# Side-by-side merges and one pass per head in a neighbourhood-attention and delta-rule layer

## The chip, the cores and the metric

The kernel runs on one core of a Trainium2 chip. The metric is device time in microseconds (us), the median of several runs. Inside the core PE is the matrix engine (TensorE), PEld its loading of the stationary operand, DVE the vector engine, ACT the scalar engine, POOL the GpSimd engine, and SP the queue that issues nearly all DMAs. PSUM is the accumulator memory that PE writes; it has eight banks of 512 floats in each of 128 partitions. L701 is line 701 of the kernel.

## What is computed

One layer over 1024 latent tokens (a grid of 16 rows by 64 columns) of width 1024, with 256 context tokens. The projection `w_in` is 1024 x 4112, the output projection `w_out` 1024 x 1024, all in float32. The reference, cut to what matters and with its einsums shortened (`hc` is projected in the same way and gives the context's keys, values and chunks):

```python
h  = rmsnorm(x, g_pre) * (1.0 + scale[:, None]) + shift[:, None]
hc = rmsnorm(xc, g_pre) * (1.0 + scale_c) + shift_c
na_q, na_k, na_v, na_z, g_qkv, g_z, g_b, g_a = jnp.split(h @ w_in, IN_SPLITS, axis=-1)
...

# neighbourhood attention, 8 heads of 64, for each row r of the grid:
s_loc = jnp.einsum('bchd,bicjhd->bhcij', q_r, k_win) + bias      # a window of 8 x 16 keys
s_ctx = jnp.einsum('bchd,bnhd->bhcn', q_r, k_ctx)                # all 256 context keys
p = jax.nn.softmax(jnp.concatenate([s_loc, s_ctx], axis=-1), axis=-1)
o_na = p_loc . v_win + p_ctx . v_ctx

# gated delta rule, 4 heads of 128, both directions, the context's chunks first:
t_inv = triangular_solve(eye + a, eye)                           # one inverse for each chunk
v_new = u_n - w_n @ state
o_n   = q_n @ state + qk_n @ v_new
state = state * gl_n + k_n^T @ v_new

y = jnp.concatenate([o_na * silu(na_z), rmsnorm(o_g, gdn_norm_w) * silu(g_z)], -1) @ w_out
return x + gate[:, None] * rmsnorm(y, g_post)
```

## The kernel before

The kernel is one program in four stages.

**Front.** Norm and modulation of `x`, the projections that the delta rule needs, its convolutions, and the first groups of small inverses. The change does not touch it.

**Projections and merges (`phase_a2`).** The rest of the `w_in` projections run on PE as products of two-part operands: each float32 matrix is held as a high part in the fast float32 format and a low part, and a product is three matmuls (high by high, low by high, high by low). The generator `fill` issues them, `pz` (the gates) last. Beside it two other generators are advanced by turns: `blocks` (the last group of 32 x 32 inverses) and `merges`. For each of the four heads `inv_merge` builds the inverse of 10 chunks of 128 in both directions `d` from four 32 x 32 inverses each. It loads the off-diagonal blocks `pm` and the small inverses `vd`, transposes `vd` into `ld`, copies the small inverses to the diagonal of the zeroed results `tm[0]` and `tm[1]` (and into `xo`), and then does two levels of "multiply, copy from PSUM, multiply, negate into place": `tz` (L1108), `zt`, `tu` (L1122) on blocks of 32, and `tz2` (L1136), `z2`, `tu2` (L1142, L1144) on blocks of 64. At the end both `tm` are stored to `tm_dram`. A head is done before the next begins. There are three `tm` buffers and each head takes two, so from head 1 on a `tm` has to wait for a store of the head before. Even heads put `pm` into the buffers `kk0`, `kk1` of the pool `pf`, in which the first pair of attention heads will be held; so `blocks` waits for all four merges (`len(ready) < 4`) before it issues the load of that pair.

**Attention and scan (`phase_b`).** Attention works on 4 pairs of heads x 2 row tiles `rt` x 4 column tiles `ct`, two heads `hh` each: 64 heads' tiles of 128 queries. `na_scores` adds bias and mask to `gm` on POOL (L729), puts the scores of the context into a PSUM tile `pc` (L736) and those of the neighbourhood's rows into another, `pl` (L739); each has its bank, with two buffers. DVE takes the maximum over `pc` (L744) and then, in one custom pass over `pl` and `gm` (L745), writes the biased scores and extends the maximum; ACT does the two exponentials with their sums (L746, L747). `na_turn` transposes the weights back into the same PSUM tiles (L754, L758), ACT copies `tcx` (L756), DVE copies `tl` (L760). `na_values` accumulates `po` (L769, L774). Between the steps of attention the delta rule's scan (`delta_step`, 4 heads x 10 chunks) is advanced by a fixed ratio. PE's order here is fixed: `self.pe` ties every matmul to the one before. The other engines' orders come from a scheduler that follows the order of the program.

**Output projection (`phase4`).** `w_out` is loaded in eight rows of 128 x 1024 in the order `W_ORDER`, in halves (`wor`), and each half is split into a high part on ACT and a low part on POOL (L701). That begins during attention: `w_out_early` takes over buffers that attention and the scan have finished with, four rows ahead. `m` is the gated result, in eight rows too. The products (L1337, L1338, L1339) go row by row over seven PSUM tiles. `last` holds the scan's end for head 3 (`delta_end`: normalisation at L1284, four transposes `ot` at L1287, twice).

The lines that set the orders and buffers that the prediction speaks of:

```python
W_ORDER = [3, 0, 1, 2, 4, 5, 6, 7]
...
tm = [g3.tile([P, 10, P], F32, name=f"tm{h}_{d}", tag="tm", bufs=3) for d in range(2)]
...
while done < min(118, (i + 1) * 118 // 130):
    next(sc)
...
banks = {"sc": 2, "sl": 2, "po": 1, "pa0": 1, "pa1": 1, "os": 1}
```

## Time and profile before

| | |
|---|---|
| median of 3 runs | 890.77 us |
| the three runs | 889.36, 890.77, 899.58 us |
| the profiled execution | 898.68 us, of which its span is 896.9 |
| mean granted PE clock | 0.962 |
| moved by DMA | 160.97 MB, mean 179 GB/s |

How to read the rows that follow. The page gives for each engine its busy time, its share of the span and the number of its instructions; then the span in 40 slices, with the busy tenths of each slice and under `PEclk` the tenths of full clock that PE was granted. A table of stretches has start and end in us, the length, then busy time and count of PE, PEld, DVE, ACT and POOL, then PE's busy share, its clock and what the DMAs moved in GB/s (the prediction names the last columns where it uses them). The chain of waits has start, length, engine and operation, in order of time, followed back from the last instruction. A group of instructions has line, engine, operation, output and inputs, shapes and count, then busy us, mean ns of one, and the idle time of the engine just ahead of them with what ended most of it. A wait has who waited, for whom, the us, the number of waits, and the longest.

The kernel's time by stages: the front to 460 us, projections and merges to 556, attention and scan to 797, output projection to the end at 897.

### The profile page before, as it was taken

Reading aid. Unit: us, or ns where it says so; the run is one execution under the profiler, and the core shown is the slowest. Engines: PE = TensorE matmul, PEld = TensorE weight load, DVE = VectorE, ACT = ScalarE, POOL = GpSimd, SP = SyncE. Lnnn points to the kernel's source line nnn. Section 1 sums busy time; section 2 is a strip of 40 time slices with the busy share of each in tenths; the row PEclk is TensorE's granted clock in tenths of the full one; section 3 lists DMA queues with packets and bytes.
Section 4 is the critical chain, followed back from the end, with each engine's and each line's share of the span. In section 5 each row is a group of like instructions: output and inputs, shape, how many; then the busy total and the mean of one; then the engine's idle time right before and its main releaser. Section 6 shows DMA issues by size and latency. Waiting matters only on the chain.

```text
span 896.9 us, 16578 instructions
## 1 busy us (share of the span) xinstructions
PE 837.1 (93%) x6082; PEld 704.4 (79%) x6082; DVE 542.1 (60%) x1179; ACT 416.9 (46%) x1165; POOL 352.8 (39%) x415
## 2 busy tenths in 40 slices
PE   6999999999999979898989997899899999989996
PEld 4678887888788858688877876788788888868885
DVE  3453454556536699779649433577677787781332
ACT  4253535745653554563143533556455555661210
POOL 1333221734453442345512112646546566643110
PEclk9899999999999999999998986799999999989999
DMA  9687442265365535743899857978829523251251
GB/s 339 248 284 253 131 127 85 83 217 169 106 200 174 151 100 176 196 107 93 299 259 253 214 189 288 347 169 217 301 77 294 160 80 133 71 193 66 96 183 51
DMA packets 95175, 160.97 MB, mean 179 GB/s; under 512 B 28581, under 2 KB 55542, under 8 KB 92918
## 3 DMA queue, kind: packets, MB, share of 16 engines
q1 hardware_dynamic: 87606, 146.25, 52.5%
q10 hardware_dynamic: 7488, 13.67, 4.9%
q8 instruction: 48, 0.79, 0.4%
q14 instruction: 33, 0.27, 0.1%
HBM read 110.82 MB, written 52.42 MB: 182 GB/s over the span
## 4 chain that ended last, share of the span: by engine, by line
PE 61%; DVE 19%; DMA 11%; ACT 3%; issue 3%; SPq 2%; POOL 1%; DVEq 0%; POOLq 0%; ACTq 0%
PE py L1337 3%; PE py L1339 3%; PE py L1338 3%; DVE tb L1063 3%; DVE vb L1066 3%; PE pz L461 2%; PE pz L465 2%; PE pz L466 2%; DMA pm_dram<-pm 2%; PE pl L739 2%; PE po L774 2%; PE po L769 2%; PE pa L1228 2%; PE pc L736 2%; DMA tm_dram<-tm 2%
## 5 line engine op out<-in xcount | busy, mean ns | idle before, releaser
L729 POOL TENSOR_TENSOR gm<-gt,mk 128x288 f32<-128x288 f32 (+1 forms) x48 | 46.3, 969 | 40.4 <-DVE nm L745 40.4
L1204 POOL TENSOR_SCALAR kd<-kt,kd 128x128 f32<-128x128 f32 x72 | 42.7, 604 | 28.0 <-PE pa L1239 27.9
L746 ACT ACTIVATE pt<-pt,nm 128x288 f32<-128x288 f32 (+1 forms) x64 | 36.7, 574 | 30.2 <-DVE nm L745 29.9
L760 DVE COPY tl<-pl 96x384 f32<-96x384 f32 (+1 forms) x64 | 35.3, 552 | 17.3 <-PE pl L758 16.4
L745 DVE CUSTOM_DVE_ANT_0 pt<-pl,gm,mi 128x288 f32<-128x288 f32 (+1 forms) x64 | 36.3, 567 | 11.0 <-POOL gm L729 4.7
L1005 ACT ACTIVATE em<-em,gc 128x128 f32<-128x128 f32 x80 | 25.6, 391 | 34.3 <-DMA em<-gc_dram 29.3
L465 PE MATMUL pz<-hl,wh_gz 128*128 128x512 f32 x96 | 39.9, 415 | 0.0
L466 PE MATMUL pz<-hh,wl_gz 128*128 128x512 f32 x96 | 39.5, 412 | 0.0
L461 PE MATMUL pz<-hh,wh_gz 128*128 128x512 f32 x96 | 39.4, 410 | 0.0
L474 PE MATMUL pv<-wh_nv,hh 128*128 128x264 f32 x128 | 35.7, 298 | 2.0 <-ACT hh L263 1.6
L1208 POOL TENSOR_SCALAR vb<-v,beta 128x128 f32<-128x128 f32 x40 | 24.2, 606 | 32.6 <-DVE y L1212 16.7
L475 PE MATMUL pv<-wh_nv,hl 128*128 128x264 f32 x128 | 36.9, 293 | 0.0
L476 PE MATMUL pv<-wl_nv,hh 128*128 128x264 f32 x128 | 35.9, 290 | 1.0 <-DVE wl_nv L447 1.0
L1391 ACT ACTIVATE finv<-py 128x512 f32<-128x512 f32 x16 | 9.6, 599 | 57.3 <-PE py L1339 39.1
L1063 DVE TENSOR_TENSOR tb<-ab,vb 120x31 f32<-120x31 f32 (+15 forms) x62 | 30.2, 487 | 9.9 <-DMA ab<-ab_dram 8.3
L872 DVE SCALAR_TENSOR_TENSOR acc_v<-xp_v,cols,acc_v 128x1282 f32<-128x1282 f32 x16 | 29.1, 1818 | 10.9 <-ACT acc_v L870 10.6
L1392 DVE TENSOR_TENSOR finv<-py,ggb 128x512 f32<-128x512 f32 x16 | 11.0, 690 | 40.6 <-ACT finv L1391 40.5
L744 DVE TENSOR_REDUCE mi<-pc 128x1 f32<-128x256 f32 x64 | 26.9, 420 | 12.4 <-PE pc L736 11.6
L1024 POOL TENSOR_SCALAR_AFFINE_SELECT qe<-qe 128x256 f32<-128x256 f32 x32 | 24.2, 759 | 24.7 <-DVE qe L1023 24.3
L758 PE MATMUL pl<-c,pt 128*96 128x128 f32 (+1 forms) x192 | 32.1, 277 | 0.0
L1020 DVE SCALAR_TENSOR_TENSOR pm<-pk,beta,em 128x128 f32<-128x128 f32 x80 | 23.6, 343 | 13.1 <-PE pk L1013 10.9
L872 DVE SCALAR_TENSOR_TENSOR acc_q<-xp_q,cols,acc_q 128x1024 f32<-128x1024 f32 x16 | 20.5, 1284 | 17.0 <-ACT acc_q L870 16.7
(433 smaller groups left out, 2907.5 us busy)
## 6 DMA issues: line engine op xcount, KB each, us to landing
wada<-in_w_ada SPq DMA_DIRECT2D x16, 512.0 KB, 6.9
em<-gc_dram SPq DMA_DIRECT2D x20, 256.0 KB, 4.1
pm_dram<-pm SPq DMA_DIRECT2D x20, 256.0 KB, 3.2
pmf<-pm_dram SPq DMA_DIRECT2D x8, 640.0 KB, 7.0
tm_dram<-tm SPq DMA_DIRECT2D x8, 640.0 KB, 7.5
kk<-qk_dram SPq DMA_DIRECT2D x16, 320.0 KB, 9.1
tm<-tm_dram SPq DMA_DIRECT2D x4, 1280.0 KB, 16.1
kq_dram<-kq SPq DMA_DIRECT2D x4, 1152.0 KB
```

The lines of the kernel that those rows point to most:

```text
L461: r = nc.tensor.matmul(ps, wh, xh, start=(k == 0), stop=False)
L465: nc.tensor.matmul(ps, wh, xl, start=False, stop=False)
L466: nc.tensor.matmul(ps, wl, xh, start=False, stop=(k == KC - 1))
L474: nc.tensor.matmul(ps, xh, wh, start=(k == 0), stop=False)
L475: nc.tensor.matmul(ps, xl, wh, start=False, stop=False)
L476: nc.tensor.matmul(ps, xh, wl, start=False, stop=(k == KC - 1))
L729: nc.gpsimd.tensor_tensor(self.gm[hh][:, :n].rearrange("p (n c r) -> p n c r", c=nco, r=4), gv, self.mk[:, mo:mo + n].rearrange("p (n c r) ...
L745: nc.vector.tensor_tensor_reduce(pt[:, :n], pl[:, :n], gm[:, :n], -1.0, mi, ALU.add, ALU.min, nm)
L746: nc.scalar.activation(pt[:, :n], pt[:, :n], AF.Exp, bias=nm, scale=-1.0, accum_out=sums[:, ct, hh, 0:1])
L872: nc.vector.scalar_tensor_tensor(av, xp[:, s0 + tap:s0 + tap + 1282 - s0], wc(tap), av, ALU.mult, ALU.add)
L1063: nc.vector.tensor_tensor(t3, bc(ab[:, 0:m, m:m + 1], [r, m, n]), bc(vb[:, m:m + 1, m:], [r, m, n]), ALU.mult)
L1204: nc.gpsimd.tensor_scalar(kd[d], kt_[:, t, :], self.kd[:, h, d, t:t + 1], None, ALU.mult)
```

## The change

Four things are changed together.

1. **Merges side by side.** `inv_merge` is cut into five stages, and the table `MERGES` interleaves the stages of neighbouring heads. `tm[1]` is allocated a stage later than `tm[0]`, its four diagonal copies go from ACT to POOL, and the order of the copies changes. For even heads `ld`, `xo`, `zt` are now also put into the first pair's buffers (`ql0`, `qh1`, `ql1`) beside `pm` in `kk0`, `kk1`. The first pair's load is issued when three merges are done. The ring of `tm` stays at three.
2. **One pass per head.** Scores of rows and context lie side by side in one PSUM tile of two banks, rows ending at column 512 and context behind it, two buffers. One custom DVE pass runs over both (288 + 256 or 384 + 256 columns); the separate maximum is gone. `gm` becomes three lasting tiles with zeros under the context's columns. One exponential with one sum replaces two. All five transposes are issued ahead of the copies. `tcx` and `tl` have three buffers instead of four.
3. **The start of the scan.** The first step's `kd` and `vb` on POOL are ordered behind the `gm` issued by then, and the scan is advanced by `1 + max(0, i - 2) * 117 // 127` steps instead of `(i + 1) * 118 // 130`.
4. **The output projection's start.** `W_ORDER` begins with row 0. Rows 0 and 3 of `w_out` and row 0 of `m` are split during attention into the first pair's buffers, row 1 of `w_out` into `o` and `tm`: three rows of `w_out` ahead instead of four. A piece is split at the earliest two steps after it was issued for loading (`clock`). The scan's end is issued at the third row of products instead of the fifth.

```diff
@@ -134,7 +134,9 @@
-W_ORDER = [3, 0, 1, 2, 4, 5, 6, 7]
+MERGES = [(0, 0), (0, 1), (1, 0), (0, 2), (1, 1), (0, 3), (0, 4), (2, 0), (1, 2), (2, 1), (1, 3), (1, 4), (3, 0), (2, 2), (3, 1),
+          (2, 3), (2, 4), (3, 2), (3, 3), (3, 4)]
+W_ORDER = [0, 3, 1, 2, 4, 5, 6, 7]
...
@@ -607,6 +609,9 @@
+        self.gms, self.gmi = [self.nw.tile([P, 640], F32, name=f"gm{i}") for i in range(3)], 0
+        for g in self.gms:
+            nc.gpsimd.memset(g[:, 384:], 0.0)
...
@@ -644,15 +647,21 @@
             if p == 2:
-                self.wait_w = 6
-                self.w_out_early(self.pf, [("qh0", 8), ("ql0", 8), ("qh1", 8), ("ql1", 8), ("kk0", 10), ("kk1", 10)])
+                self.clock += 4
+                w = [self.pf.tile([P, n], F32, name=f"early_{t}", tag=t)[:, :D]
+                     for t, n in (("qh0", S), ("ql0", S), ("qh1", S), ("ql1", S), ("kk0", S + CT), ("kk1", S + CT))]
+                self.split_w(W_ORDER[0], *w[:2])
+                self.split_w(W_ORDER[1], *w[2:4])
+                self.ms[0] = tuple(v.bitcast(F32R) for v in w[4:])
+                self.split_later(self.m_dram[0:P, :], *w[4:])
+                self.clock -= 4
...
@@ -665,38 +674,33 @@
-            self.split_piece()
+            self.split_piece(1, 2)
...
+    def split_piece(self, n=1, wait=0):
+        nc = self.nc
+        self.clock += 1
+        for _ in range(n):
+            if not self.staged or self.clock - self.staged[0][0] < wait:
+                return
+            _, raw, hi, lo = self.staged.pop(0)
             self.order(nc.scalar.copy(hi.bitcast(F32R), raw), self.last_exp)
             nc.gpsimd.tensor_tensor(lo.bitcast(F32R), raw, hi, ALU.subtract)
             self.load_pieces()
@@ -725,39 +729,39 @@
         if ct != 2:
-            self.gm[hh] = self.nw.tile([P, 384], F32, name=f"gm{p}_{u}_{hh}", tag="gm", bufs=3)
-            nc.gpsimd.tensor_tensor(self.gm[hh][:, :n].rearrange("p (n c r) -> p n c r", c=nco, r=4), gv,
+            self.gm[hh] = self.gms[self.gmi % 3]
+            self.gmi += 1
+            r = nc.gpsimd.tensor_tensor(self.gm[hh][:, 384 - n:384].rearrange("p (n c r) -> p n c r", c=nco, r=4), gv,
                                     self.mk[:, mo:mo + n].rearrange("p (n c r) -> p n c r", c=nco, r=4), ALU.add)
+            self.last_gm = r.ins.name
         gm = self.gm[hh]
-        pc = ps.tile([P, 512], F32, name=f"pc{p}_{u}_{hh}", tag="sc", bufs=2)[:, :256]
-        pl = ps.tile([P, 512], F32, name=f"pl{p}_{u}_{hh}", tag="sl", bufs=2)
+
+        sc = ps.tile([P, 1024], F32, name=f"sc{p}_{u}_{hh}", tag="sc", bufs=2)
+        pl, pc = sc[:, :512], sc[:, 512:768]
...
-            self.pe(nc.tensor.matmul(pl[:, :n].rearrange("p (n f) -> p n f", f=m), a[:, u * P:(u + 1) * P], kv,
+            self.pe(nc.tensor.matmul(pl[:, 512 - n:].rearrange("p (n f) -> p n f", f=m), a[:, u * P:(u + 1) * P], kv,
                                      start=(i == 0), stop=(i == 1)))
-        mi = self.nw.tile([P, 1], F32, name=f"mi{p}_{u}_{hh}", tag="mi", bufs=4)
...
-        nc.vector.tensor_reduce(mi, pc, AX.X, ALU.max, negate=True)
-        nc.vector.tensor_tensor_reduce(pt[:, :n], pl[:, :n], gm[:, :n], -1.0, mi, ALU.add, ALU.min, nm)
-        nc.scalar.activation(pt[:, :n], pt[:, :n], AF.Exp, bias=nm, scale=-1.0, accum_out=sums[:, ct, hh, 0:1])
-        self.last_exp = nc.scalar.activation(pt[:, 384:640], pc, AF.Exp, bias=nm,
-                                             accum_out=sums[:, ct, hh, 1:2]).ins.name
+        nc.vector.tensor_tensor_reduce(pt[:, 384 - n:], sc[:, 512 - n:768], gm[:, 384 - n:], -1.0, 3.0e38, ALU.add, ALU.min, nm)
+        self.last_exp = nc.scalar.activation(pt[:, 384 - n:], pt[:, 384 - n:], AF.Exp, bias=nm, scale=-1.0,
+                                             accum_out=sums[:, ct, hh:hh + 1]).ins.name
...
     def na_turn(self, nm, m, pc, pl, pt):
...
-        tcx = self.nw.tile([P, 2, P], F32, name=f"tcx{nm}", tag="tcx", bufs=4)
+        for rc in range(3):
+            self.pe(nc.tensor.transpose(pl[:m, (rc + 1) * P:(rc + 2) * P], pt[:, 384 + (rc - 3) * m:384 + (rc - 2) * m], self.ident))
+        tcx = self.nw.tile([P, 2, P], F32, name=f"tcx{nm}", tag="tcx", bufs=3)
...
@@ -1072,34 +1076,35 @@
     def inv_merge(self, g3, ps, h):
...
+        pm = [buf(f"pmf{d}_", f"pm{d}", [10, P], f"kk{d}") for d in range(2)]
...
-        tm = [g3.tile([P, 10, P], F32, name=f"tm{h}_{d}", tag="tm", bufs=3) for d in range(2)]
...
+        yield
+
+        ld, xo, zt = buf("ld", "ld", [2, 10, 32], "ql0"), buf("xo", "xo", [10, 64], "qh1"), buf("zt", "zt", [2, 10, 32], "ql1")
+        tm = [g3.tile([P, 10, P], F32, name=f"tm{h}_0", tag="tm", bufs=3)]
         nc.gpsimd.memset(xo, 0.0)
-        yield
+        nc.gpsimd.memset(tm[0], 0.0)
...
         yield
+        tm.append(g3.tile([P, 10, P], F32, name=f"tm{h}_1", tag="tm", bufs=3))
+        nc.gpsimd.memset(tm[1], 0.0)
+        for b in range(4):
+            sl = slice(32 * b, 32 * b + 32)
+            nc.gpsimd.tensor_copy(tm[1][sl, :, sl], ld[sl, 1])
...
-        yield
         for d in range(2):
             nc.sync.dma_start(self.tm_dram[h][:, d], tm[d])
+        yield
...
@@ -1183,7 +1200,10 @@
                 if (h, i) == (3, 1):
-                    self.w_out_early(g3, [("o", 8), ("tm", 20)])
+                    w = [g3.tile([P, n, P], F32, name=f"early_{t}", tag=t, bufs=2).rearrange("p t c -> p (t c)")
+                         for t, n in (("o", 8), ("tm", 20))]
+                    self.spare = w[1][:, D:2 * D]
+                    self.split_w(W_ORDER[2], w[0], w[1][:, :D])
...
+                if (h, i) == (0, 0):
+                    self.order(r, self.last_gm)
...
-        banks = {"sc": 2, "sl": 2, "po": 1, "pa0": 1, "pa1": 1, "os": 1}
-        tags = [tag for tag, n in banks.items() for _ in range(n)]
+        tags = ["sc", "sc", "sc", "sc", "po", "pa0", "pa1", "os"]
...
                     next(parts, None)
+                    self.split_piece(2)
+                    if i == 2:
+                        for _ in last:
+                            pass
...
-                    if i == 4:
-                        for _ in last:
-                            pass
-                        self.split_piece(6)
...
-                while len(ready) < 4:
+                while len(ready) < 3:
...
+                heads = [self.inv_merge(ap, ps, h) for h in range(4)]
+                for h, stage in MERGES:
+                    while stage == 0 and (8 * h + 7) // 12 not in self.yd:
                         yield
-                    yield from self.inv_merge(ap, ps, h)
-                    ready.append(h)
+                    next(heads[h])
+                    if stage == 4:
+                        ready.append(h)
...
-                    while done < min(118, (i + 1) * 118 // 130):
+                    while done < min(118, 1 + max(0, i - 2) * 117 // 127):
```

What that does to the order of instructions is shown at three places. The first is PE at the end of the projections. Before, the rows around the last projection matmul (`pz_1`, L466), and then, after head 3's `tu`, those up to the first scores (`pc`, L736); `pmf_0` and `pmf_1` are head 3's off-diagonal blocks, `z` its `z2`:

```order
L466 MATMUL pz_1_5673<-hh,wl_gz_4_5640 128x512
L1122 MATMUL tu_0_5369<-vd_5297,zt_5322 32x32
...
L1136 MATMUL tz_00_5469<-xo_5305,pmf_0_5293 64x64 x5
L1136 MATMUL tz_05_5476<-xo_5305,pmf_0_5293 64x64 x5
L1136 MATMUL tz_10_5483<-tm_1_5304,pmf_1_5295 64x64 x5
L1142 MATMUL tu_00_5497<-tm_0_5303,z_5468 64x64 x5
L1136 MATMUL tz_15_5490<-tm_1_5304,pmf_1_5295 64x64 x5
L1144 MATMUL tu_10_5498<-z_5468,xo_5305 64x64 x5
L1142 MATMUL tu_05_5511<-tm_0_5303,z_5468 64x64 x5
L1144 MATMUL tu_15_5512<-z_5468,xo_5305 64x64 x5
L736 MATMUL pc_0_0_5723<-kk_0_5266,qh_0_5269 128x256
```

After, the last projection is L468, and `pmf_2` are head 2's blocks:

```order
L468 MATMUL pz_1_5673<-hh,wl_gz_4_5640 128x512
L1153 MATMUL tz_00_5262<-xo_4897,pmf_2_4766 64x64 x5
L1159 MATMUL tu_00_5290<-tm_0_4899,z_5261 64x64 x5
...
L1161 MATMUL tu_15_5305<-z_5261,xo_4897 64x64 x5
L1139 MATMUL tu_0_5326<-vd_5092,zt_5173 32x32
L1139 MATMUL tu_0_5326<-zt_5173,vd_5092 32x32
...
L1153 MATMUL tz_00_5438<-xo_5172,pmf_3_5088 64x64 x5
...
L1161 MATMUL tu_15_5481<-z_5437,xo_5172 64x64 x5
L743 MATMUL sc_0_0_5728<-kk_0_5061,qh_0_5064 128x256
```

Before, only head 3's second half stands behind the last projection. Now the second half of head 2 stands there too, and behind it head 3's from `tu` (L1139) on; head 2 ends in the middle.

The second place is POOL at the start of attention. Before, with `vb` and `kd` the operands of the scan's first steps and `gm` the bias tiles of attention:

```order
L1091 MEMSET tm_1_5304 128x1280
L1208 TENSOR_SCALAR vb_1_1_5774<-v_5737,beta 128x128
L1208 TENSOR_SCALAR vb_1_0_5819<-v_5737,beta 128x128
L1208 TENSOR_SCALAR vb_1_9_5887<-v_5737,beta 128x128
L1204 TENSOR_SCALAR kd_0_0_5770<-kt_5738,kd 128x128
L1204 TENSOR_SCALAR kd_1_1_5772<-kt_5738,kd 128x128
L1204 TENSOR_SCALAR kd_0_1_5812<-kt_5738,kd 128x128
L729 TENSOR_TENSOR gm_0_0_5721<-gt_0_5284,mk 128x288
```

After, from the zeroing of head 3's second `tm` on:

```order
L1127 MEMSET tm_1_5320 128x1280
L1130 COPY tm_1_5320<-ld_5171 32x10x32 x4
L614 MEMSET gm_5718 128x256
L614 MEMSET gm_5719 128x256
L614 MEMSET gm_5720 128x256
L734 TENSOR_TENSOR gm_5718<-gt_0_5079,mk 128x288
L734 TENSOR_TENSOR gm_5719<-gt_1_5081,mk 128x288
L734 TENSOR_TENSOR gm_5720<-gt_0_5079,mk 128x384
L1224 TENSOR_SCALAR kd_0_0_5785<-kt_5739,kd 128x128
L1224 TENSOR_SCALAR kd_1_1_5787<-kt_5739,kd 128x128
L1230 TENSOR_SCALAR vb_1_1_5789<-v_5738,beta 128x128
```

The first three `gm` went ahead of the scan's operands, and the copies into head 3's `tm[1]` and three short memsets came in ahead of them.

The third place is PE at the start of the output projection. Before, from the last scan product (`pos`, L1250) to the first product of the projection (`py`, L1337):

```order
L1250 MATMUL pos_8485<-vn_0_9_9085,qe_7703 128x128
L1250 MATMUL pos_8485<-vn_1_2_9088,qe_7703 128x128
L754 MATMUL pc_7_1_9042<-c_60,pt_7_1_9050 128x128 x2
L758 MATMUL pl_7_1_9043<-c_60,pt_7_1_9050 96x128 x3
L769 MATMUL po_1_8844<-tcx_7_1_9104,vcx 64x128
...
L774 MATMUL po_1_8844<-tl_7_0_9080,vv_7632 64x128
L637 MATMUL prt_1_9139<-c_60,rb_1_9137 128x128 x4
L1287 MATMUL ot_0_9295<-c_60,o_8314 128x128 x4
L1337 MATMUL py_0_9167<-wo_o_8360,m_9145 128x512
```

After:

```order
L1274 MATMUL pos_8250<-vn_0_9_8780,qe_7534 128x128
L1361 MATMUL py_1_8866<-early_qh_8151,early_kk_8155 128x512
L1362 MATMUL py_1_8866<-early_qh_8151,early_kk_8156 128x512
L1363 MATMUL py_1_8866<-early_ql_8152,early_kk_8155 128x512
L1274 MATMUL pos_8250<-vn_1_2_8783,qe_7534 128x128
L758 MATMUL sc_7_1_8743<-c_60,pt_7_1_8749 128x128 x2
L760 MATMUL sc_7_1_8743<-c_60,pt_7_1_8749 96x128 x3
L1361 MATMUL py_0_8867<-early_qh_8151,early_kk_8155 128x512
...
L778 MATMUL po_1_8565<-tl_7_0_8777,vv_7440 64x128
...
L640 MATMUL prt_1_8833<-c_60,rb_1_8831 128x128 x4
L1311 MATMUL ot_0_8960<-c_60,o_8076 128x128 x4
```

The first products, of row 0 (`early_qh`, `early_ql`, with `early_kk` as `m`), now stand between the last scan products, the last transposes and the scan's end, and the two `ot` follow each other closely.

99 lines of the change are left out of this document (46 added, 53 removed).

## The prediction

> **What bounds the kernel now.** I read the page's totals and slices first, then a table of stretches, then the chain of waits in order of time, then the groups by form, and last the timeline at the seams.
>
> ```profile
> span 896.9 us, 16578 instructions
> PE 837.1 (93%) x6082; PEld 704.4 (79%) x6082; DVE 542.1 (60%) x1179; ACT 416.9 (46%) x1165; POOL 352.8 (39%) x415
> PEclk9899999999999999999998986799999999989999
> ```
>
> PE is busy nearly throughout, and the only dip of its clock lies in the slices between about 500 and 580 us. The table of stretches (length; busy time and count of each engine; clock; DMA) shows the seams:
>
> ```profile
> 460.00:542.00 82.00, 76.93 (x1114) 62.59 (x1113) 47.90 (x103) 38.47 (x84) 13.02 (x12) 0.90 0.81 228
> 542.00:556.00 14.00, 9.60 (x203) 8.93 (x202) 5.24 (x11) 4.10 (x9) 1.17 (x1) 0.64 0.65 233
> 556.00:571.00 15.00, 9.99 (x54) 9.38 (x55) 6.07 (x18) 4.99 (x18) 9.97 (x14) 0.54 1.01 400
> 571.00:797.00 226.00, 209.74 (x1927) 186.96 (x1923) 171.12 (x532) 133.65 (x490) 132.87 (x179) 0.99 0.60 175
> 797.00:885.00 88.00, 88.00 (x373) 71.15 (x374) 34.20 (x47) 19.84 (x43) 15.62 (x21) 0.97 0.35 121
> ```
>
> The last projections and the merges end at 542, a tail of merges runs to 556, attention starts at half clock, runs to 797, and the output projection follows without a gap. So what can be won is: the tail and the start (29 us at a clock of 0.64 and 0.54), the weight loader's idle time in attention (226 - 187 = 39 us), and the seam at 790 to 805. The work before 440 us is not touched.
>
> **The merges.** The chain in order of time (start, length, what), from the end of head 0 to the first scores:
>
> ```profile
> 489.69 0.79 PE tu L1142 x10
> ...
> 496.87 1.39 PE tu L1122 x100
> ...
> 500.07 0.23 PE pk L461
> ...
> 501.70 1.30 PE tz L1136 x20
> ...
> 514.00 9.28 DMA tm_dram<-tm
> ...
> 537.64 4.99 DMA tm_dram<-tm
> ...
> 542.74 1.18 POOL tm L1091
> 543.93 0.46 ACT tm L1099
> ...
> 545.83 0.61 ACT st_z L553
> ...
> 547.06 0.47 DVE tm L1127
> ...
> 548.19 3.11 PE tz L1136 x27
> ...
> 555.70 0.72 PE pc L736 x2
> ```
>
> Each head ends with the store of its `tm`, and a later head's `tm` waits for that store, since there are three buffers. Head 2's store at 537.64 is followed by the memset, four copies, the negations and two passes until 555.70: 18.1 us for one handover. Heads 0 and 1 end at about 491 and 513.
>
> The new order runs heads 0 and 1 together, then 2 and 3, but the ring still has three buffers in the same roles: head 2's second `tm` waits for head 1's store, head 3's for head 2's. In PE's order head 0 ends after 22 more projection matmuls (22 x 0.23 = 5.1 us) and beside head 1's first passes, where it had waited before; I put its end at 495. From there to head 1's end stand 75 projection matmuls (17.3 us) and passes of about 4 us; with 2 us of waits, 518. Then two handovers follow with only 15 projection matmuls between them. One costs: the store, 5.0 to 9.3 us by the two rows, taken as 7 because `kk` and `ql` loads are now issued just ahead of it; the memset 1.2; four copies, now on POOL, estimated at 2.0 from ACT's 4 x 0.46; a negation 0.5; and 4.5 of the 7.5 us between 548.19 and 555.70, since the first direction no longer stands behind `st_z` in DVE's queue. That is 15.2, so scores start at 518 + 30.4 = 548.4 against 555.7: **7 us** sooner. Bounds: stores of 5.0 and no waits give 13; stores of 9.3 give 0.7, and head 0 ending at 500 on top gives -4. The loads moved behind (`ql_1`, `kk`, `ql_0`, `qh_1`) land under head 3's handover; if one of them came last it would cost its excess over that 15 us.
>
> The Trainium skill, "TensorE: Matmul & The Clock Gate", section "What's actually happening", says that PE runs at half clock unless it has been busy for a window of about 3.4 us, and falls back after an idle one. The rows agree (0.64 and 0.54 where PE waits for stores), and it speaks against this change, since the part without projections under it grows. By that rule the tail's passes are cold, as I priced them; with the warm passes of 1.39 and 1.30 us a handover would be some 3 us shorter and the gain 13.
>
> **The start of attention.** POOL's timeline, PE's wait, and the chain:
>
> ```profile
> 556.30 1.21 POOL L1208 TENSOR_SCALAR vb<-v,beta 128x128 f32<-128x128 f32 x2 [12.40 <-DMA v<-vt_dram]
> 561.06 4.70 POOL L729 TENSOR_TENSOR gm<-gt,mk 128x288 f32<-128x288 f32 x5
> ...
> PE pc L754 <- ACT pt L747: 5.0, 1, 5.0
> ...
> 570.37 0.59 PE po L769 x8
> ```
>
> POOL's bias tiles `gm` stood behind `vb` and `kd`, which waited for the scan's `v`, and PE waited 5.0 us for the first exponentials. Now three short memsets and three `gm` stand first, and the scan's first two steps wait for them instead; they need nothing that lands late. The first transposes then come a pass and an exponential (0.78 + 0.75, below) after the first scores, of which the second scores hide about 1.1: a wait of some 0.8 remains. Gain **4 us**; bounds 0 (`gm` still last, because POOL now also makes head 3's copies) and 5.0, plus up to 4 if the clock recovers sooner.
>
> **One pass per head.** The groups by form (busy, mean ns), and the weight loader's waits in attention:
>
> ```profile
> L744 DVE TENSOR_REDUCE mi<-pc 128x1 f32<-128x256 f32 x64 | 26.9, 420 | 12.4 <-PE pc L736 11.6
> L745 DVE CUSTOM_DVE_ANT_0 pt<-pl,gm,mi 128x384 f32<-128x384 f32 x32 | 19.8, 617 | 3.8 <-DVE mi L744 0.9 <-ACT vn L1233 0.7 <-PE pa L1210 0.5
> L745 DVE CUSTOM_DVE_ANT_0 pt<-pl,gm,mi 128x288 f32<-128x288 f32 x32 | 16.5, 517 | 7.2 <-POOL gm L729 4.7 <-DVE mi L744 0.7 <-ACT osq L1267 0.7
> L746 ACT ACTIVATE pt<-pt,nm 128x384 f32<-128x384 f32 x32 | 19.6, 614 | 17.4 <-DVE nm L745 17.4
> L746 ACT ACTIVATE pt<-pt,nm 128x288 f32<-128x288 f32 x32 | 17.1, 535 | 12.9 <-DVE nm L745 12.5
> L747 ACT ACTIVATE pt<-pc,nm 128x256 f32<-128x256 f32 x64 | 29.2, 457 | 0.0
> L747 ACT ACTIVATION_READ_ACCUMULATOR pt<-pc,nm 128x1 f32 x64 | 12.3, 192 | 0.0
> ...
> PEld pc L736 <- ACT tcx L756: 7.6, 15, 0.9
> PEld pl L739 <- DVE tl L760: 4.6, 12, 0.7
> ```
>
> A pass over 544 or 640 columns is not in the trace. From 288 to 384 columns DVE grows by 100 ns (1.04 ns a column) and ACT by 79 (0.82), so the pass costs 783 or 883 and the exponential 746 or 825. DVE saves 420 + 517 - 783 = 154 ns a head, 9.9 us over 64; ACT saves 535 + 457 + 192 - 746 = 438, 28 us. Neither engine bounds; what counts is PE's wait for `tcx`, which ACT copies only after the next head's exponentials. From the end of the scores that chain was 617 + 614 + 192 + 457 = 1.88 us (the maximum ran under the second scores) and is 883 + 825 = 1.71, with one accumulator read fewer behind it: 0.2 to 0.35 sooner. It is felt about once in a pair of heads, 32 x 0.25 = **8 us**, about the 7.6 of the row. Against it: rows and context now share a tile, so the context scores wait for `tl` too: 12 such waits grow by up to 0.36 (the half-clock 0.72 above, halved), 4 us. Bounds: -4, and 39 (the loader's idle time); I stay at 8, near the wait that the edit shortens. Three buffers of `tcx` and `tl` instead of four cost nothing, as the values of a pair are read before its successor's second copy; if not, it is one wait as in the 4.6 row.
>
> **The output projection's start.** The timeline there:
>
> ```profile
> 789.59 0.71 PE L1250 MATMUL pos<-vn,qe 128*128 128x128 f32 x4
> ...
> 795.16 3.45 DVE L1284 TENSOR_TENSOR o<-o,rq_y_o 128x512 f32<-128x512 f32 x2
> ...
> 796.97 1.11 PE L1287 MATMUL ot<-c,o 128*128 128x128 f32 x4 [2.63 <-DVE o L1284]
> ...
> 804.30 0.40 PE L1339 MATMUL py<-wo_tm,m 128*128 128x512 f32 x1
> ...
> L701 POOL TENSOR_TENSOR fintm<-wor,fintm x2: 1559/1680/1800, 803.4 to 806.7; 128x512 fp32r<-128x512 f32 x2
> ```
>
> From the last scan product (790.3) to the end of the first weight row (804.7) PE does about 2.9 us of transposes and values and 21 x 0.23 = 4.8 us of products: 6.7 of 14.4 us are lost. Now row 0, already split, comes first, and 18 of its products (4.1 us) fill the wait for the scan's end. What is late next is `zs`: its DVE product stands behind the 3.45 us of L1284, and the `po` bank and row 3 wait for it, about 2.5 us. Gain **4 us** (bounds 1.5 and 6.7). Three rows of `w_out` are split ahead instead of four; three rows of products (14.5 us) cover the fourth's two pieces, at 1.7 us of POOL each, and if they came too slowly it would cost about 1 us a row. The DMAs are as many.
>
> **Sum.** 7 + 4 + 8 + 4 = 23 us. The profiled execution took 898.7 us (its span and 1.8 around it), so one like it would take 875.7. The median of the runs is 890.8, 7.9 below; from it the sum gives 868.
>
> **The rivals.**
> The merges give nothing: the handovers are serial as before and each store takes the 9.28 us of the first. For: the same ring, and nothing under the last 30 us. Against: two heads now share 17 us of projections. Then 890.8 - 16 = 875.
> Attention does not move: PE's loader waits for `tl` and `kd` where it waited for `tcx`. For: the new coupling. Against: both queues get shorter. Then 890.8 - 15 = 876.
> Slower: the two-bank tile makes DVE the bound. If each next score had to wait for a `tl` copy that stands behind a whole pass (0.83 on average), 64 x 0.83 = 53 us less the 15 of the other terms is 929. It decides against the change from 0.51 us a head on ((17.8 + 15) / 64). For: DVE is the busiest feeder, 171 of 226 us. Against: only 12 such waits now, 4.6 us in all, and DVE has 10 us less to do.
>
> **Chances.** 2% (17.8 us) is about what a measurement of this kernel tells from no change. The forecast has 0.62; its own spread, from the bounds, puts 0.54 below 873 and 0.08 above. Merges 0.17 and attention 0.15 end within 2%; the DVE bound has 0.05; 0.01 is for more gain than the bounds of the middle terms. So faster 0.55, same 0.40, slower 0.05. For 8 in 10 the range runs from 853 (the tail at 13 and attention at 17) to 885 (both at nothing and 9 lost elsewhere).
>
> **What would show it.** First scores near 548 instead of 555.7 and two stores about 15 us apart before them; no 5 us wait at the first transposes; the loader's wait for `tcx` under 3 us and for `tl` not over 9; products of row 0 between the last scan products. Wrong would be: scores after 556, a new wait of the scores for DVE on every head, or waits for `raw` pieces in the output projection.

## The result, and the profile after

The changed kernel takes 928.83 us (median of 4 runs, 926.28 to 929.62), the kernel before beside it 892.0 us: a ratio of 1.0394, with a 95% interval of 1.0326 to 1.0461. It is slower by 37 us. The profiled execution took 929.62 us; that of the kernel before took 898.68, some 7 above its median, so the two traces differ by 31 us only, and that difference is split up below. Of the four executions of `two_tiles`, among the experiments, one ran at a granted clock of 0.746 and took 1015.69 us; it is left out there.

The page of the changed kernel (span; busy time, share and count of each engine; PE's clock by slice):

```profile
span 927.9 us, 16429 instructions
PE 837.4 (90%) x6082; PEld 701.9 (76%) x6082; DVE 531.3 (57%) x1106; ACT 395.1 (43%) x1022; POOL 364.2 (39%) x436
PEclk9999999999999999999999867999999999999999
```

PE does the same work in the same busy time as before (837 us), DVE and ACT do 11 and 22 us less, and the span is 31 us longer. So PE waits. The table of stretches of the changed kernel shows where:

```profile
542.00:557.00 15.00, 7.98 (x78) 7.57 (x79) 3.30 (x7) 1.68 (x4) 6.55 (x11) 0.50 1.02 324
557.00:571.00 14.00, 11.62 (x72) 9.96 (x70) 5.74 (x15) 4.98 (x13) 6.84 (x11) 0.63 1.02 421
571.00:830.00 259.00, 217.23 (x1925) 189.74 (x1925) 158.13 (x460) 117.48 (x366) 131.76 (x179) 1.00 0.52 154
830.00:916.00 86.00, 83.59 (x359) 67.36 (x358) 34.98 (x47) 21.81 (x45) 18.86 (x24) 0.98 0.38 127
```

Attention ran from 571 to 797 before and runs from 571 to 830 now. Four marks that both traces have, all on PE, split the difference (us):

| from | to | before | after | difference |
|---|---|---|---|---|
| start | first scores | 555.6 | 557.4 | +1.8 |
| first scores | first values (`po`) | 14.7 | 10.9 | -3.8 |
| first values | last row transposes (`pt`) | 220.1 | 256.5 | +36.4 |
| last row transposes | end of span | 106.5 | 103.1 | -3.4 |

The whole loss lies inside attention. Who waited there for whom (engine and line, the us in all, the number, the longest), first the matmuls in attention, then their weight loads:

```profile
PE sc L743 <- DVE tl L764: 37.3, 51, 1.5
```

```profile
PEld sc L743 <- DVE tl L764: 49.4, 55, 1.7
```

The scores of the context, the first access to a score tile, wait for the copy `tl` at 51 to 55 of the 64 heads, for 0.7 to 0.9 us each. Before, the largest such entry on the loader was 7.6 us, for `tcx`. The other end of the same loop is DVE, which waits for the scores:

```profile
DVE pt L750 <- PE sc L746: 32.8, 40, 1.2
```

DVE does not have too much to do: it is busy for 158 of 259 us. PE waits for DVE, and DVE for PE. One head of each kernel shows the loop, by the timelines. Before, from the transposes of a head to the next scores:

```profile
674.26 0.38 PE L754 MATMUL pc<-c,pt 128*128 128x128 f32 x2
674.48 0.49 PE L758 MATMUL pl<-c,pt 128*96 128x128 f32 x3
...
674.68 0.37 ACT L756 COPY tcx<-pc 128x256 f32<-128x256 f32 x1
...
675.01 0.55 DVE L760 COPY tl<-pl 96x384 f32<-96x384 f32 x1
...
675.63 0.36 PE L736 MATMUL pc<-kk,qh 128*128 128x256 f32 x1
...
675.95 0.29 PE L739 MATMUL pl<-kk,qh 128*128 128x288 f32 x1
```

After:

```profile
690.72 0.38 PE L758 MATMUL sc<-c,pt 128*128 128x128 f32 x2
...
690.90 0.75 ACT L751 ACTIVATE pt<-pt,nm 128x544 f32<-128x544 f32 x1
690.93 0.49 PE L760 MATMUL sc<-c,pt 128*96 128x128 f32 x3
...
691.65 0.35 ACT L762 COPY tcx<-sc 128x256 f32<-128x256 f32 x1
...
692.18 0.54 DVE L764 COPY tl<-sc 96x384 f32<-96x384 f32 x1
...
692.77 0.39 PE L743 MATMUL sc<-kk,qh 128*128 128x256 f32 x1 [0.90 <-DVE tl L764]
```

Before, `tcx` and `tl` do not wait for each other: the one waits for its own two transposes, the other for its own three, and the context's scores need `tcx` alone. After, they follow each other. `tcx` waits for all five transposes (and, as before, stands behind an exponential on ACT); `tl` starts when `tcx` is done; the scores start when `tl` is done, here 1.35 us after the last transpose instead of 0.66. All 64 heads show it: in the timelines `tl` starts a median of 0.12 us after `tcx` has ended, and the time from the end of a head's last transpose to the end of `tl` adds up to 84.5 us, against 46.2 before. The compiled programs say the same: all 64 copies `tl` waited for PE's semaphore before, and wait for ACT's now, although the two copies read different banks; and the context's scores of 62 heads waited for ACT's (`tcx`) before, and wait for DVE's (`tl`) now. So here the second reader of the shared tile is put behind the first. One of DVE's rows in each program, before and after:

```text
L760 COPY tl_0_0_8337<-pl_0_0_8239 96x384 [waits PE_49]
L764 COPY tl_6_0_7906<-sc_6_0_7826 128x384 [waits Activation_49]
```

The durations that the prediction had worked out are there (groups by form):

```profile
L750 DVE CUSTOM_DVE_ANT_0 pt<-sc,gm 128x640 f32<-128x640 f32 x32 | 26.4, 825 | 25.9 <-PE sc L746 25.3 <-POOL vb L1230 0.6
...
L751 ACT ACTIVATE pt<-pt,nm 128x544 f32<-128x544 f32 x32 | 24.0, 749 | 30.3 <-DVE nm L750 29.9
```

Of the merges, the timelines of the changed kernel show on SP the stores of heads 0, 1 and 2 (L1166) and the loads ahead of head 3's `pmf`, on PE the wait that holds up head 1, and on POOL the wait of head 3's second `tm`:

```profile
500.38 0.84 SPq L1166 DMA_DIRECT2D tm_dram<-tm  x2
...
507.83 3.03 SPq L1099 DMA_DIRECT2D vd<-yd  x4
510.91 2.87 SPq L156 DMA_DIRECT2D vv<-v_dram  x3
513.88 0.42 SPq L1095 DMA_DIRECT2D pmf<-pm_dram  x1
...
528.58 1.01 SPq L1166 DMA_DIRECT2D tm_dram<-tm  x2
...
540.26 1.02 SPq L1166 DMA_DIRECT2D tm_dram<-tm  x2
```

```profile
520.42 1.27 PE L1113 MATMUL tz<-ld,pmf 32*32 32x32 f32 x40 [2.58 <-DMA pmf<-pm_dram]
```

```profile
550.11 1.17 POOL L1127 MEMSET tm<- 128x1280 f32 x1 [13.99 <-DMA tm_dram<-tm]
```

In PE's order the second half of head 1's last pass (L1159, L1161) stands behind head 3's first pass (L1113) and 14 projection matmuls. Head 3's `pmf` goes into head 1's buffer, whose first half PE had read by 510.6. SP issued the load at 513.88 only, behind the loads of `vd` and `vv`, which it issued without a wait between; it landed 6.4 us later. PE waited for it, and head 1's store came at 528.58.

The start of attention and of the output projection, by the waits of PE in the first and by PE's timeline in the second:

```profile
PE sc L758 <- ACT pt L751: 0.9, 1, 0.9
```

```profile
831.37 0.66 PE L1311 MATMUL ot<-c,o 128*128 128x128 f32 x4 [0.76 <-DVE o L1308]
833.67 0.79 PE L1361 MATMUL py<-early_qh,early_kk 128*128 128x512 f32 x1 [1.64 <-DVE zs L642]
```

The wait of 5.0 us at the first transposes is 0.9 us, and the wait of 2.63 us at the seam to the output projection has become 0.76, with one of 1.64 behind it.

### The profile page after: what moved, and what is told of

Same layout as the page of the kernel before. It is cut to its first block, busy times and chain, and to the rows that moved or that the text cites. A ratio compares the mean times of both kernels' runs of the same rounds, so it can differ in the third digit from the quotient of the medians.

```text
span 927.9 us, 16429 instructions
## 1 busy us (share of the span) xinstructions
PE 837.4 (90%) x6082; PEld 701.9 (76%) x6082; DVE 531.3 (57%) x1106; ACT 395.1 (43%) x1022; POOL 364.2 (39%) x436
## 4 chain that ended last, share of the span: by engine, by line
PE 55%; DVE 21%; DMA 13%; issue 4%; ACT 3%; SPq 3%; POOL 1%; DVEq 0%; POOLq 0%; ACTq 0%
DMA qe<-qe_dram 3%; PE py L1361 3%; PE py L1362 3%; PE py L1363 3%; DVE tb L1067 3%; DVE vb L1070 3%; DVE tl L764 2%; PE sc L743 2%; PE pz L467 2%; PE pz L463 2%; PE pz L468 2%; DMA pm_dram<-pm 2%; PE po L778 2%; PE sc L746 2%; PE po L773 1%
## 5 line engine op out<-in xcount | busy, mean ns | idle before, releaser
L751 ACT ACTIVATE pt<-pt,nm 128x544 f32<-128x544 f32 (+1 forms) x64 | 50.5, 789 | 79.5 <-DVE nm L750 79.0
L750 DVE CUSTOM_DVE_ANT_0 pt<-sc,gm 128x544 f32<-128x544 f32 (+1 forms) x64 | 49.5, 774 | 41.6 <-PE sc L746 36.3
L743 PE MATMUL sc<-kk,qh 128*128 128x256 f32 x64 | 25.0, 390 | 38.2 <-DVE tl L764 37.3
L743 PEld LDWEIGHTS sc<-kk,qh 128*128 128x128 f32 x64 | 12.3, 192 | 49.5 <-DVE tl L764 49.4
L764 DVE COPY tl<-sc 96x384 f32<-96x384 f32 (+1 forms) x64 | 35.2, 550 | 10.1 <-ACT tcx L762 9.8
L468 PE MATMUL pz<-hh,wl_gz 128*128 128x512 f32 x96 | 38.9, 405 | 0.0
L1423 DVE TENSOR_TENSOR finv<-py,ggb 128x512 f32<-128x512 f32 x16 | 10.9, 689 | 48.2 <-ACT finv L1422 48.1
L1266 DVE SCALAR_TENSOR_TENSOR s<-s,egl,pa 128x128 f32<-128x128 f32 x64 | 20.5, 343 | 28.6 <-PE pa L1263 28.6
L876 DVE SCALAR_TENSOR_TENSOR acc_v<-xp_v,cols,acc_v 128x1282 f32<-128x1282 f32 x16 | 29.1, 1817 | 10.9 <-ACT acc_v L874 10.6
L760 PE MATMUL sc<-c,pt 128*96 128x128 f32 (+1 forms) x192 | 32.1, 277 | 0.0
L1024 DVE SCALAR_TENSOR_TENSOR pm<-pk,beta,em 128x128 f32<-128x128 f32 x80 | 23.6, 343 | 14.4 <-PE pk L1017 10.9
## 6 DMA issues: line engine op xcount, KB each, us to landing
tm_dram<-tm SPq DMA_DIRECT2D x8, 640.0 KB, 10.2
```

What stands on the lines that cost most here:

```text
L468: nc.tensor.matmul(ps, wl, xh, start=False, stop=(k == KC - 1))
L743: self.pe(nc.tensor.matmul(pc, a[:, u * P:(u + 1) * P], kk[:, S:S + CT], start=(i == 0), stop=(i == 1)))
L750: nc.vector.tensor_tensor_reduce(pt[:, 384 - n:], sc[:, 512 - n:768], gm[:, 384 - n:], -1.0, 3.0e38, ALU.add, ALU.min, nm)
L751: self.last_exp = nc.scalar.activation(pt[:, 384 - n:], pt[:, 384 - n:], AF.Exp, bias=nm, scale=-1.0, accum_out=sums[:, ct, hh:hh + 1]).in ...
L764: nc.vector.tensor_copy(tl[:m, :], pl[:m, P:])
```

## The experiments

Each was timed beside the kernel before on the same chip; the ratios are to that kernel.

**Two tiles again in the changed kernel (`two_tiles`).** The one pass per head is undone, all else stays.

```diff
-        sc = ps.tile([P, 1024], F32, name=f"sc{p}_{u}_{hh}", tag="sc", bufs=2)
-        pl, pc = sc[:, :512], sc[:, 512:768]
+        pc = ps.tile([P, 512], F32, name=f"pc{p}_{u}_{hh}", tag="sc", bufs=2)[:, :256]
+        pl = ps.tile([P, 512], F32, name=f"pl{p}_{u}_{hh}", tag="sl", bufs=2)
...
-        nc.vector.tensor_tensor_reduce(pt[:, 384 - n:], sc[:, 512 - n:768], gm[:, 384 - n:], -1.0, 3.0e38, ALU.add, ALU.min, nm)
+        nc.vector.tensor_reduce(mi, pc, AX.X, ALU.max, negate=True)
+        nc.vector.tensor_tensor_reduce(pt[:, :n], pl[:, :n], gm[:, :n], -1.0, mi, ALU.add, ALU.min, nm)
```

> The changed kernel with the scores of rows and context in two PSUM tiles again, two passes and two exponentials as before; merges, POOL's order, pacing of the scan, buffers of tcx, tl and y and the output projection stay changed. Theory A (the shared tile and the one pass carry the whole loss; the three other parts together gained 1.75 - 3.8 - 3.4 = -5.4 us by the two traces): about 886, 883 to 891; first values to last transposes back from 256 to 220 us. Theory B (the scan's pacing or the three instead of four buffers slow attention): 910 or more.

902.69 us, ratio 1.0119 (1.0076 to 1.0163). Neither theory: 26 us of the 37 went, 11 stayed. PE's waits for `tl` fell to 2.7 us, but a wait stood there that neither kernel had to this extent:

```profile
PE pos L1276 <- DMA qe<-qe_dram: 8.7, 2, 4.8
PE pc L742 <- ACT tcx L762: 5.7, 12, 0.9
PE pl L745 <- DVE tl L766: 2.7, 8, 0.5
```

SP's timeline shows why. Before, at a change of the scan's heads:

```profile
620.20 0.33 SPq L154 DMA_DIRECT2D tm<-tm_dram  x1
621.37 0.32 SPq L154 DMA_DIRECT2D qe<-qe_dram  x1
...
623.92 0.32 SPq L154 DMA_DIRECT2D kq<-kq_dram  x1
```

With two tiles and the rest of the change:

```profile
615.14 0.61 SPq L156 DMA_DIRECT2D tm<-tm_dram  x1
616.55 0.32 SPq L156 DMA_DIRECT2D kq<-kq_dram  x1
...
618.93 0.32 SPq L156 DMA_DIRECT2D qe<-qe_dram  x1
```

`qe` had come ahead of `kq`, and now comes behind it: the chain of waits gives it 15.77 us from issue to use. Behind each of the two waits the granted clock is 0.85 (634 to 650 and 697 to 720), where `two_pace`, below, has 1.00. The changed kernel has this order too, but there attention was so late that only 2.0 us of it were felt.

**The waits alone, in the kernel before (`b_chain`, `b_release`, `b_both`).** Tiles, passes and exponentials stay as before; only semaphore waits are added that the shared tile brings.

```diff
+    def sync(self, r, before):
+        self.tc.add_manual_dep(r.ins, before, mybir.DependencyInfo(mybir.DependencyClass.Sync,
+                               mybir.DependencyReason.DATA), reason="as in one tile")
...
+            if i == 0 and self.n_sc > 1:
+                self.sync(r, self.tls[self.n_sc - 2])
...
+        r = nc.vector.tensor_copy(tl[:m, :], pl[:m, :384])
+        self.sync(r, c.ins.name)
```

The first `sync` makes the context's scores wait for `tl` (`b_release`), the second makes `tl` wait for `tcx` (`b_chain`).

> The kernel before with one wait added: the copy tl on DVE waits for the copy tcx on ACT of the same head, as it does in the shared tile. Nothing else changes. Theory A1 (the serial copies are the main cost): 12 to 30 us slower than before. Theory A2 (the context's scores waiting for tl are the main cost): within 6 us of before. Theory C (the longer pass is the main cost): within 6 us.

> The kernel before with one wait added: the context's scores of a head wait for the copy tl of the head two earlier, as they do in the shared tile. Theory A2: 12 to 30 us slower than before. Theory A1: within 10 us. Theory C: within 6 us.

> The kernel before with both waits: tl after tcx, and the context's scores after tl. Two tiles, two passes and two exponentials stay. Theory A (both waits of the shared tile carry the loss): 25 to 36 us slower than before, about the 36 us of the trace. Theory C (the longer pass of 0.77 us on DVE, not the waits): at most 12 us slower.

| | us | ratio | interval |
|---|---|---|---|
| `b_chain` | 904.38 | 1.0120 | 1.0081 to 1.0159 |
| `b_release` | 900.54 | 1.0086 | 1.0061 to 1.0111 |
| `b_both` | 918.5 | 1.0285 | 1.0246 to 1.0323 |

Each costs 8 to 12 us by itself, and both 26, some 6 more than their sum. Part of the 6 is a load: in `b_both` too SP issues `qe` behind `kq` at the first change of heads, and PE waits 4.5 us for it, against 0.9 before. The rest fits the copies: where the scores wait for `tl` and `tl` waits for `tcx`, the two lie on PE's path in a row. PE's waits for them are 5.7 us before, 9.6 and 10.2 with one wait added, and 22.0 with both. Theory C, by which the longer pass does it, is out for the most part, since no pass is longer here. PE's waits in `b_both`:

```profile
PE pc L740 <- DVE tl L768: 22.0, 30, 1.3
...
PE pos L1260 <- DMA qe<-qe_dram: 4.5, 1, 4.5
```

**The second part of the change alone (`b_onepass`).** The kernel before with shared tile, one pass, one exponential, and the smaller buffer counts that make room.

> The kernel before with the second part of the change alone: shared tile, one pass, one exponential, three buffers of tcx and tl and two of y (four and three don't fit beside the wider bias tiles). Merges, pacing, POOL's order and output projection as before. If the two waits of the shared tile are all (26 us when added to the kernel before), 26 us slower than before, 22 to 30. If the longer pass costs something on top, 32 us slower or more. If the shorter DVE and ACT work gives something back, under 20.

926.26 us, ratio 1.0384 (1.0326 to 1.0441): 33 us, within the intervals the whole effect of the change. The two waits, put into the kernel before, made 26.

**The third wait (`b_three`).** `b_both`, and `tcx` also waits for the row transposes.

```diff
+        c = nc.scalar.copy(tcx.rearrange("p c q -> p (c q)"), pc)
+        self.sync(c, r.ins.name)
```

> b_both (the kernel before with tl after tcx and the context's scores after tl, 26 us slower) with the third wait of the shared tile added: tcx waits for all five transposes of its head, not for its own two. Two passes, two exponentials and four buffers stay. If the waits of the shared tile carry the whole 33 us of b_onepass: 30 to 36 us slower than before, 922 to 929. If the longer pass carries the rest: within 4 us of b_both, 915 to 922.

934.97 us, ratio 1.0459 (1.0403 to 1.0514): 41 us, more than expected. With all three waits of the shared tile in place, two passes are 8.7 us slower than the one pass of `b_onepass`. PE's waits, first of `b_three`, then of `b_onepass`:

```profile
PE pc L740 <- DVE tl L770: 37.1, 52, 1.9
...
PE pos L1262 <- DMA qe<-qe_dram: 2.7, 1, 2.7
```

```profile
PE sc L740 <- DVE tl L761: 31.4, 49, 1.7
```

So the waits alone make as much waiting (37.1 us) as the changed kernel has (37.3), and with the single pass beside them it is some 6 us less (31.4). 2.7 us of the 8.7 may be the load of `qe`, which `b_onepass` does not wait for, and the intervals overlap a little. In the traces, from the first scores to the last row transposes, `b_three` takes 276 us and `b_onepass` 266. That the pass itself costs nothing is well supported; that it gives 6 to 9 us is likely.

**The scan's pacing (`two_pace`, `after_pace`).**

```diff
-                    while done < min(118, 1 + max(0, i - 2) * 117 // 127):
+                    while done < min(118, (i + 1) * 118 // 130):
```

> two_tiles with the scan's pacing of before, (i + 1) * 118 // 130. Theory D (with the new pacing SP issues qe behind v and kq, so the scan waits 8.7 us for qe at two heads and PE's clock drops behind it): 8 to 14 us less than two_tiles, about 892, 889 to 896, and waits for qe under 3 us. Rival (the three buffers of tcx and tl, or POOL's order): within 4 us of two_tiles, 900 to 908.

> The changed kernel with the scan's pacing of before. Its waits for qe were only 2.0 us, since attention itself was late. Theory A (shared tile): within 5 us of the changed kernel, 923 to 931. Rival (the pacing puts the scan's work where attention cannot use it): under 915.

`two_pace` took 893.33 us, ratio 0.9997 (0.9971 to 1.0023), 9 to 11 us less than `two_tiles` (by the medians and by the ratios); its wait for `qe` is 1.1 us, and SP issues `qe` ahead of `kq` again. `after_pace` took 924.67, ratio 1.0351 (1.0310 to 1.0393), some 4 us less than the changed kernel, with intervals that overlap. Its trace has no wait for `qe` and less waiting for `tl`, as little as `b_onepass`, which has the same pacing:

```profile
PE sc L743 <- DVE tl L764: 31.1, 49, 1.7
```

So the pacing costs about 10 us where attention is fast, and perhaps 4 where it is slow, and without it and the shared tile the rest of the change is worth nothing that can be measured. The pacing is not all that sets the order of `qe` and `kq`: `b_both` and `b_three` have the pacing of before, and there too `qe` comes behind `kq` once.

**One copy instead of two (`one_copy_dve`).**

```diff
-        tcx = self.nw.tile([P, 2, P], F32, name=f"tcx{nm}", tag="tcx", bufs=3)
-        nc.scalar.copy(tcx.rearrange("p c q -> p (c q)"), pc)
-        tl = self.nw.tile([P, 384], F32, name=f"tl{nm}", tag="tl", bufs=3)
-        nc.vector.tensor_copy(tl[:m, :], pl[:m, P:])
...
+        tl = self.nw.tile([P, 640], F32, name=f"tl{nm}", tag="tl", bufs=3)
+        nc.vector.tensor_copy(tl, sc[:, P:768])
```

> The changed kernel with tl and tcx copied by one DVE instruction of 640 columns instead of one on ACT and one on DVE; the row transposes take 128 columns, so that all partitions are written, and the values read the same part. By the 0.55 us for 384 columns the copy takes about 0.9 us, as long as the two in a row (0.37 + 0.55). Theory A1a (only the sum of the two copies between the transposes and the next scores counts): within 7 us of the changed kernel, 922 to 936. Theory A1b (it counts that tcx stands behind an exponential of 0.8 us in ACT's queue): 8 to 20 us less, 909 to 921.

914.95 us, ratio 1.0250 (1.0197 to 1.0302): 14 us less than the changed kernel. The group of the copy, by form:

```profile
L762 DVE COPY tl<-sc 128x640 f32<-128x640 f32 x64 | 52.4, 819 | 22.0 <-PE sc L760 21.7
```

By the timelines the time from a head's last transpose to the end of its last copy adds up to 68.1 us, 16.4 less than in the changed kernel. The copying itself is 6.2 us less (819 ns against 365 and 550), and the handover from ACT to DVE, 9.6 us over the 64 heads, is gone. The wait ahead of the first copy stayed, 15.9 us against 16.5: the one copy now stands behind DVE's other work where `tcx` stood behind an exponential. So the time lies in the range of theory A1b, but not for its reason. PE's wait for `tl` fell from 37.3 to 19.3 us:

```profile
PE sc L743 <- DVE tl L762: 19.3, 32, 1.5
```

**More time behind the transposes (`after_late`, `two_late`, `b_late`).** The values move from ahead of a head's transposes to behind them.

```diff
-            if i >= 3 and i % 2:
-                values((i - 3) // 2)
             yield
             if 1 <= i <= 2 * len(units):
                 turned[divmod(i - 1, 2)] = self.na_turn(*scores.pop(i - 1))
+            if i >= 3 and i % 2:
+                values((i - 3) // 2)
```

> The changed kernel with one order on PE changed: the values of a pair (1.25 us of PE work, every second head) are issued behind the transposes of a head instead of ahead of them, so that they stand between the transposes and the next scores. Theory A (the wait is for the time that the serial copies take behind the transposes): half of the 51 waits of 0.73 us go, 12 to 20 us less, 909 to 917. Rival (the rate of DVE, 158 of 259 us busy, or its pass bounds): within 6 us of the changed kernel. The first exponential behind each score has less cover, which would cost up to 5.

> two_pace with the values issued behind the transposes, as in after_late. With two tiles the scores' waits for tcx and tl are only 5.7 us, so at most 4 us less, 889 to 893; up to 6 us more if the exponentials lose their cover.

> The kernel before with the values issued behind the transposes, nothing else. Its scores' waits for tcx and tl were 5.7 us in all: if two_late's 2.8 us less than two_pace come from there, 888 to 892; otherwise 892 to 896.

`after_late`, in the changed kernel: 909.19 us, ratio 1.0178 (1.0135 to 1.0222), 20 us less. The number of waits fell from 51 to 29, and what they hold from 37.3 us to 26.4 (on the loader from 49.4 to 33.4). That accounts for 11 to 16 of the 20 us:

```profile
PE sc L743 <- DVE tl L764: 26.4, 29, 2.4
```

`two_late`, on `two_pace`: 890.56 us, ratio 0.9962 (0.9936 to 0.9988), the lowest ratio of all, 0.4% under the kernel before. `b_late`, on the kernel before: 890.63 us, ratio 0.9991 (0.9965 to 1.0017), which can't be told from no change; nor, with these intervals, from `two_late`.

**All three repairs in the changed kernel (`one_late_pace`).** One copy, late values, the pacing of before.

> The changed kernel with the three repairs together: one copy of 640 columns on DVE, the values behind the transposes, the scan's pacing of before. Alone they took 14, 20 and 4 us off 929. If they add up for the most part: 893 to 900, level with before; if the pass then also gives back what it saves on DVE and ACT, under 890; if the shared tile's release still bounds, over 903.

905.72 us, ratio 1.0151 (1.0112 to 1.0189). They add up to 23 of the 38 that they took singly. By the number that is the third case, over 903, but the release of the tile can no longer be most of the 13 us over the kernel before: PE's wait for `tl` is down to 6.8 us. Others have come up, for a copy on ACT and for the scan's `o`; what else there is was not found:

```profile
PE sc L743 <- DVE tl L762: 6.8, 14, 1.1
PE pa L1261 <- ACT vn L1253: 4.7, 3, 4.0
PE pos L1239 <- DVE o L1280: 3.7, 6, 0.7
```

No kernel with the shared tile got below the kernel before.

**Merges one after another (`two_seq`) and four buffers (`two_b4`), both on `two_pace`.**

> two_pace with the merges one head after another as before (first part of the change undone); what is left of the change is POOL's order at the start, three buffers, the wider order of the first loads apart, and the output projection. Theory E (the side-by-side merges start attention 2 to 3.5 us later, by 557.45 and 559.17 against 555.70): 2 to 5 us less than two_pace, 888 to 891. Prediction's step (they start it 7 us earlier): 5 to 9 us more, 898 to 902.

> two_pace with four buffers of tcx and tl and three of y, as before. What is left of the change: merges, POOL's order at the start, the output projection. Theory F (the three buffers take back what the start and the output projection gain: attention from the first values on was 7.7 us longer in two_pace's trace than before): 4 to 8 us less than two_pace, 885 to 889. Rival (they cost nothing, as the prediction said): within 3 us of two_pace, 890 to 896.

`two_seq` took 892.29 us, ratio 0.9977 (0.9954 to 1.0), 1.0 less than `two_pace`: less than theory E said, and far from the 5 to 9 more of the prediction's step. `two_b4` took 896.83, ratio 1.0033 (0.9999 to 1.0067), just over the rival's range, so the smaller buffer counts cost nothing that shows and theory F is out.

## Why the prediction was wrong

**The merges: 7 us sooner, measured none.** The two handovers came out as costed in their sum: 28.9 us from head 1's store (528.58) to the first scores (557.4), against 30.4, though one took 11.7 and the other 17.2 where 15.2 had been put for each. The step that failed is the one before, "and passes of about 4 us; with 2 us of waits, 518" for head 1's end. Head 0's last pass left PE at 497.5, not 495, and its store came at 500.38. From 497.5 to the end of head 1's last pass at 528.1 are 30.6 us, where 23.3 had been put (17.3 of projections, 4, 2). The projection matmuls had been counted rightly, but 11 of them, behind the wait of 2.58 us for `pmf`, took 0.43 us each instead of 0.23, 2.2 us in all; and the passes took 7.3 us instead of 4. The wait for `pmf` was not listed: head 3's load goes into head 1's buffer and stood behind other loads on SP.

By the clock the new order is worth 1.0 us less than the old one (`two_seq`), within the uncertainty. The traces lean to a loss: the first scores came at 547 to 559 us in eight kernels with the old merges (mean 551.6) and at 553 to 561 in nine with the new (mean 556.9), but kernels with the same code up to there differ by as much as 12 us, so this stays open. The 555.7 that the prediction started from is itself late among the eight.

The Trainium skill, "TensorE: Matmul & The Clock Gate", section "What's actually happening", has PE at half clock after an idle window, which spoke against this change. The row agrees: the granted clock between 542 and 557 is 0.50, where it was 0.64. (The 0.54 that the prediction also gave to waits for stores belongs to the start of attention, where PE waited 5.0 us for the first exponentials.)

**The start of attention: 4 us, measured 3.8 by the marks of the trace.** Right, and by the step named: the wait of 5.0 us became 0.9, as `gm` no longer stands behind `vb` and `kd`.

**One pass per head: 8 us gained, measured 33 lost (`b_onepass`; the 36 of the marks hold the pacing too).** The step that failed is "rows and context now share a tile, so the context scores wait for `tl` too: 12 such waits grow by up to 0.36", 4 us. I carried the count of waits over from the kernel before, where `tcx` and `tl` do not wait for each other. In the shared tile there are 51 to 55 waits of 0.7 to 0.9 us, because the wait of the scores for `tl`, which the working had, comes with two that it did not have: `tl` for `tcx`, and `tcx` for the row transposes. Put into the kernel before without anything else, the first two cost 26 us and all three 41. The gain side was sound: the pass came out at 723 and 825 ns where 783 and 883 had been worked out, the exponential at 749 and 828 where it was 746 and 825, and with the same waits the single pass is likely some 6 to 9 us faster than two. The working priced what each engine has to do and for how long, not on which semaphore each instruction waits.

The slow rival gave 929, and 928.8 was measured, with a chance of 0.05. Its place was right, the scores waiting for a `tl` at every head, and its point of decision of 0.51 us a head was passed (49.4 / 64 = 0.77). Its reason was wrong: `tl` is not held up by a busy DVE (3.4 us over the 64 heads, beyond a handover of 0.15 us) but by the copy on ACT. That the number was hit is luck: it is 53 us of waits less 15 of other gains, where the runs show 33 for the tile, perhaps 4 for the pacing, and nothing for the rest.

Two of the prediction's own signs of being wrong came: scores after 556, and a new wait of the scores for DVE. Two of its bounds do not follow from its terms: stores of 9.3 leave 2.7 us of the merges' 7, not 0.7, and with the tail and attention at nothing and 9 us lost elsewhere the range would end at 892, not 885. Neither would have held 928.8.

**The scan's pacing: not costed, perhaps 4 us in the changed kernel, about 10 with two tiles.** The prediction named it nowhere. In the changed kernel and `two_tiles` `qe` comes behind `kq` on SP at both changes of heads that load both, in `after_pace` and `two_pace` ahead of it.

**The output projection: 4 us, measured 3.4 by the marks of the trace.** Right. In the kernels with two tiles and the new start of the projection the part from the last transposes to the end took 100.1 to 101.8 us, against 106.5 before. Three rows of `w_out` ahead instead of four cost nothing to be seen.

**What stays open.** `two_pace` keeps the gains at the start and behind the last transposes, 4.6 and 6.3 us by the marks of its trace, and yet equals the kernel before. Its first scores come 3.5 us later, and from the first values to the last transposes it takes 7.9 us more. Smaller buffer counts are not the reason (`two_b4`). In `two_late`, with another order of the values, first scores to last transposes take 231.9 us instead of 238.0, but the execution traced of `two_pace` was 5.7 us above its median and that of `two_late` 1.0, while the medians differ by 2.8 us; so most of this is the difference between executions. What holds PE up there in `two_pace` was not found.

## What to carry to other kernels

When two buffers were merged into one here, so that one instruction could run over both, their readers were chained and their releases joined. Before pricing the shorter instruction, list, for every engine that touches the merged tile, which semaphore it waits on in the compiled program. A wait is cheap only as long as the next user has other work between; with two buffers and a strict order on PE, the time from the last write into a tile to its release is on the path at every turn. Pacing constants of a second stream, and waits added to the first, can turn the order of the loads on the queue; look at that order whenever they move.

## What the runs showed of the hardware

A copy of 384 columns out of PSUM took DVE 550 ns and one of 640 columns 819 ns. A line through these two gives, as an estimate, 1.05 ns a column and 147 ns besides. A handover from a copy on ACT to one on DVE took a mean of 0.15 us over 64 heads of the changed kernel.
